# Half of a GELU branch moved ahead of the latent projections in a two-layer mixer kernel

## Chip, core and metric

The kernel runs on one core of a Trainium2 chip. The metric is device time in microseconds (us) of one execution, the median of several runs.

## What is computed

A two-layer network over 512 positions of 1024 channels, followed by a second block. Only layer 1's mixer matters here. It projects the normed input `h` into five pieces and feeds two branches, whose outputs are projected together:

```python
z = h @ w_in
cq, ckv, kr, xr, xg = jnp.split(z, [i1, i2, i3, i4], axis=-1)
q  = (rmsnorm(cq, g_cq) @ w_uq).reshape(Bsz, S, C_HEADS, C_NOPE + C_ROPE)
kv = (rmsnorm(ckv, g_ckv) @ w_ukv).reshape(Bsz, S, C_HEADS, C_NOPE + C_VDIM)
yc = dense_mla(qn, qr, kn, rope(kr), v)
yd = rglru_block(xr, xg, conv_w, conv_b, wa, ba, wx, bx, lam)
return jnp.concatenate([yc, yd], axis=-1) @ w_out
# in rglru_block, for both directions of the recurrence:
r, i = sigmoid(gates of conv(xr)); log_a = -8 * r * softplus(-lam[dirn])
a = exp(log_a); b = sqrt(-expm1(2 * log_a)) * (i * xcf)
h = scan(a, b);  y = (h_forward + h_backward) * gelu(xg)
```

`xr` and `xg` have 512 channels each, `cq` 256, `ckv` 128, `kr` 32. Everything is float32.

## The kernel before

Activations lie transposed: 128 channels on the partitions, 512 positions along the row. A projection block of 128 output channels is 8 chunks of input by 3 matmuls, 24 matmuls of 128x512: each float32 operand is split into a rounded part `hi` (`wh` for weights) and a rest `lo` (`wl`), and `hi*wh + hi*wl + lo*wh` is summed in one PSUM bank (`mm3`, L843). ScalarE or GpSimd makes `hi`, VectorE or GpSimd makes `lo` (`split_to`, L832). GpSimd cannot read PSUM, so what empties a bank is VectorE's or ScalarE's.

One Python program writes the instructions of all five engines in an order of its own: `_Flow` (L368) keeps a planned clock, moves it on by each matmul, and between matmuls lets the tasks that are due emit their next instructions. `_Engine.cost` (L321) holds the planned cost of an instruction, and `copy` and `tt` (L581, L591) put each on the engine that the plan expects to be free first. Tasks marked low go out only when the engines are not far behind. On the chip each engine then runs its own list strictly in order and waits on semaphores; nothing is reordered there.

Layer 1's mixer is phase "c" of the plan, started at L1779. In the order of TensorE's list:

- `xr_blocks` (L1638): four blocks of `xr`, evacuated by VectorE and convolved.
- `lru` (L1691): 16 gate products of three matmuls, each ended by a sigmoid on ScalarE. Behind them `lru_chain` (L1710) runs beside TensorE. `decay` takes two exponentials and a tanh per gate (tiles `la`, `lt`, `sg`) on ScalarE and products on VectorE or GpSimd; then come eight square roots; then `state` runs one scan per channel block and direction on VectorE (eight scans), adds both directions, multiplies by the GELU (tile `ly`) and splits the result.
- `cq.blocks` (two blocks) and `latents` (L1556: one block of `ckv`, one of `kr`). Each latent block is read by ScalarE as `hi` and as a square `sq`, and by VectorE as `lo`.
- `xg_blocks` (L1666): four blocks, each evacuated to `gz` on VectorE; the GELU is then square (ScalarE), `gt` (VectorE), tanh (ScalarE), `gz` again (VectorE).
- `mla_proj` (L1586): keys, queries and values from the latents. Each value block is scaled to `vz` on VectorE and then transposed by TensorE (`v_stack`, L937).

The latents are scaled late. `Latent.scales` (L1537) sums the squares over channels by TensorE (128x1 matmuls, tile `tr`), makes the mean on VectorE in three small instructions (`lt` 128x4), takes the power -0.5 on GpSimd (`pw` 128x4), finishes it on VectorE (`pw<-pw,pw` 128x4), and `bcast_c` (L918) then spreads it over the partitions:

```python
for b in range(NQ):
    tr(ps[:, b * P:(b + 1) * P], r.t[:, b:b + 1].to_broadcast([P, P]), ident)
yield
o.t = blk(name)
V.tensor_copy(o.t, ps)
```

The four transpositions `tr<-cst,pw` stand in TensorE's list wherever the plan expected `r.t` to be there. Nearly all instructions are issued by the helpers, so the trace shows L363 for VectorE, ScalarE and GpSimd, L561 for matmuls, L565 for transpositions. Weights come in units of 1024 columns, two for each block pair; those of this mixer are split during layer 0's MLP and written back to DRAM (`keep_ahead`, L700), and SyncE's queue fetches them (`wh<-wk`, `wl<-wk`) into four buffers in the order of `plan` (L693).

Of the kernel before, what the change touches and what calls it, by code (L numbers as in the profile page):

```python
# [367 lines left out]
class _Flow:  # L368
# [12 lines left out]
    def go(self, gen, low=False):  # L381
        t = _Task(gen, low)
        t.due = self.now + 0.1
        self.tasks.append(t)
        return t
# [89 lines left out]
def _chain(*gens):  # L475
    for g in gens:
        yield from g
# [11 lines left out]
def tile_hybrid(ctx: ExitStack, tc: tile.TileContext, wt, xT, pT, prm_d, cst_d, out):  # L489
# [4 lines left out]
    fl = _Flow()  # L494
# [19 lines left out]
    def blk(name="b", dt=F32, n=T):  # L514
        return bp.tile([P, TB], dt, tag="b", bufs=NB, name=uid(name))[:, 0:n]
# [17 lines left out]
    def take(tag):  # L533
        while (t := bank(tag)) is None:
            yield
        return t
# [6 lines left out]
    def give(tag):  # L543
        banks.append(max(fl.now, fl.last) + 0.1)
        held[tag] -= 1

    def wait(*tasks):
        for t in tasks:
            while not t.done:
                yield  # L550

    def waitc(*tasks):
        for t in tasks:
            while not t.done:
                yield 0.1
# [35 lines left out]
    def tt(op, out, a, b, bias=None):  # L591

        n = width(out)
        if PSUM in (a.space, b.space):
            e = V
        else:
            e = first((V, 0.07 + n / 960.0), (G, 0.07 + n * 0.00227 + (fl.gt if bias is None else bias)))
        e.tensor_tensor(out, a, b, op=op)
# [89 lines left out]
    def unit(name, i):  # L688
        if (name, i) not in units:
            units[name, i] = Unit(name, i, 4 if name == "ein2" else 1)  # L690
        return units[name, i]

    def plan(*names):  # L693
        for nm in names:
            for i in range((_WN[_WT[nm]][1] + 1023) // 1024):
                order.append(unit(nm, i))
# [3 lines left out]
    def keep_ahead(n, *names):  # L700

        us = iter([unit(nm, i) for nm in names for i in range((_WN[_WT[nm]][1] + 1023) // 1024)])

        def chain():
            for u in us:
                if u.task is None and u.raw is None:
                    ahead.append(u)
                    yield from u.keep()

        for _ in range(n):  # L710
            go(chain(), low=True)
# [73 lines left out]
    def PR(name, i=0, n=1):  # L785
        o, w = _PO[name]
        return prm[:, o + i:o + i + n]
# [44 lines left out]
    def split_to(act, ps, scale=None):  # L832
        act.hi, act.lo = blk("hi", F32R), blk("lo", F32R)
        yield from split_ps(ps, act.hi, act.lo, scale)
        yield
        act.done = True

    def mm3g(ps, w, b, nk, mv, m=P, bw=P, base=0, cs=slice(0, T), keep=False):
        for k in range(nk):
            yield from wait(mv[k])  # L840
            yield from mm3(ps, w, base + (b * nk + k) * bw, mv[k], k == 0, k == nk - 1, m, bw, cs, keep)
# [355 lines left out]
    def out_proj(name, yhl, h, then=None, first=None):  # L1197

        for j in range(2):
            w = weights(f"{name}{2 * h + j}")  # L1200
            for b in range(4):
                c = 4 * j + b
                if first is not None:
                    for k in range(NC) if c == 0 else (c + fl.pf,):
                        if k <= c + fl.pf and k < NC:
                            first(k)
                ps = yield from take("mm")
                yield from mm3g(ps, w, b, 4, yhl[4 * h:4 * h + 4])
                while h == 1 and (name, c) not in halves:
                    yield  # L1210
                t = go(residual(c, ps, then, halves[name, c] if h == 1 else None))
                if h == 0:
                    halves[name, c] = t
# [175 lines left out]
    def job0(hd):  # L1389
        st = {}  # L1390

        def score():
# [13 lines left out]
    h, then = next_norm(lambda c: PR("n_mlp0", c), (ss, None))  # L1406
    fill.append(out_proj("eout", yhl, 1, then))
    plan(*[f"m0_{t}_{g}_{i}" for g in range(4) for t in (1, 2) for i in range(4)])
    plan("oin0", "oin1", "lru", "oin4", "oin5", "oin2", "oin3", "ukv0", "uq0", "ukv1", "uq1",
         *[f"oout{i}" for i in range(4)])  # L1410
    fl.finish(fill)

# [56 lines left out]
    def softplus():  # L1469
# [15 lines left out]
        for k in (15, 13, 11, 9, 7, 5, 3, 1):  # L1485
# [14 lines left out]
    go(softplus())  # L1500
    go(masks("m_d4", "m_d16"))
    fl.phase("b")
    keep_ahead(2, "oin0", "oin1", "lru", "oin4", "oin5", "oin2", "oin3", "ukv0", "uq0", "ukv1", "uq1",
                  *[f"oout{i}" for i in range(4)])
    fl.run(mlp(0, h, rb, then))
    h = h2
# [49 lines left out]
    def latents():  # L1556
        yield from ckv.blocks()
        ps = yield from take("mm")
        yield from mm3g(ps, ckv.w, 1, NC, h)

        def evac():
            yield from waitc(rb)
            V.tensor_mul(tk, tk, rb.t)
            V.tensor_mul(tk, ps, tk)
            give("mm")
            yield
            t = blk("kr")
            S.activation(t[0:64], tk[64:128], AF.Copy)
            yield
            V.tensor_add(t[0:64], tk[0:64], t[0:64])  # L1570
            yield
            S.activation(t[64:128], t[0:64], AF.Copy)
            kr.t = t
            yield
            kr.done = True
            yield from waitc(cq.b)
            for i in range(2):
                tt(ALU.mult, tq[i], tq[i], cq.b.t)
            yield
            tqr.done = True  # L1580

        go(evac())
# [55 lines left out]
    def xr_blocks(i):  # L1638
        w = weights(f"oin{i}")
        for b in range(2):  # L1640
            ps = yield from take("mm")
            yield from mm3g(ps, w, b, NC, h)

            def evac(ps=ps, c=2 * i + b):
                yield from waitc(rb)
                xp = blk("xp", n=TB)
                G.memset(xp[:, 0:2], 0.0)
                G.memset(xp[:, T + 2:T + 3], 0.0)
                V.tensor_mul(xp[:, 2:T + 2], ps, rb.t)
                give("mm")  # L1650
                yield
                xc = blk("xc")
                S.activation(xc, xp[:, 0:T], AF.Identity, bias=PR("cb", c), scale=PR("cw", c))
                yield
                for j in range(1, 4):
                    V.scalar_tensor_tensor(xc, xp[:, j:j + T], PR("cw", 4 * j + c), xc,
                                           op0=ALU.mult, op1=ALU.add)
                yield
                a = _Act()
                yield from split_to(a, xc)  # L1660
                xcs[c].t = (xc, a)
                xcs[c].done = True

            go(evac())

    def xg_blocks(i):  # L1666
        w = weights(f"oin{2 + i}")
        for b in range(2):
            ps = yield from take("mm")
            yield from mm3g(ps, w, b, NC, h)  # L1670

            def evac(ps=ps, c=2 * i + b):
                yield from waitc(rb)
                z, t = blk("gz"), blk("gt")
                V.tensor_mul(z, ps, rb.t)
                give("mm")
                yield "low"
                S.activation(t, z, AF.Square, scale=math.sqrt(0.044715))
                yield
                V.scalar_tensor_tensor(t, t, 1.0, z, op0=ALU.add, op1=ALU.mult)  # L1680
                yield
                S.activation(t, t, AF.Tanh, scale=math.sqrt(2.0 / math.pi))
                yield
                V.scalar_tensor_tensor(z, t, 1.0, z, op0=ALU.add, op1=ALU.mult)
                yield
                gelu[c].t = z
                gelu[c].done = True

            go(evac())

    def lru():  # L1691
        wlru = weights("lru")
        gates, ts = {}, []
        for c in range(4):
            yield from wait(xcs[c])
            for d in range(2):
                for t, bn in ((0, "ba"), (1, "bx")):
                    ps = yield from take("mm")
                    yield from mm3g(ps, wlru, c * 4 + d * 2 + t, 1, [xcs[c].t[1]])

                    def evac(ps=ps, k=(c, d, t), b=PR(bn, 4 * d + c)):
                        gates[k] = blk("sg")
                        S.activation(gates[k], ps, AF.Sigmoid, bias=b)
                        give("mm")
                        yield

                    ts.append(go(evac()))
        go(lru_chain(gates, ts), low=True)
# [67 lines left out]
    cq = Latent(256, "oin4", 2, "g_cq", SC96)  # L1776
    ckv = Latent(128, "oin5", 1, "g_ckv", 1.0)
    fl.phase("c")
    fl.run(_chain(xr_blocks(0), xr_blocks(1), lru(), cq.blocks(), latents(), xg_blocks(0), xg_blocks(1)))  # L1779
    fill.extend([mla_proj(1), out_proj("oout", yhl, 0, first=reload(0))])  # L1780
    fl.run(mla_proj(0), fill, 0.0)
    fl.run(attend([job1(i) for i in range(8)], fl.ahead, fl.streams), fill, fl.share)
# [633 lines left out]
```

## Time and profile before

| | before |
|---|---|
| median of 3 runs (lowest, highest) | 1477.36 us (1476.55, 1479.11) |
| the profiled execution: time, span of its records | 1479.96 us, 1478.2 us |
| TensorE busy | 1449.5 us, 98% |
| VectorE busy | 899.0 us, 61% |
| ScalarE busy | 649.5 us, 44% |
| GpSimd busy | 310.7 us, 21% |
| mean granted clock of TensorE | 0.994 |

The busy share of TensorE is high nearly everywhere, so a mean says little. What counts is where its list stands still and which engine it waits for there. The mixer of layer 1 lies between 526 and about 700 us of the span.

### The profile page before, as it was taken

Reading aid. Unit: us, or ns where it says so; the run is one execution under the profiler, and the core shown is the slowest. Engines: PE = TensorE matmul, PEld = TensorE weight load, DVE = VectorE, ACT = ScalarE, POOL = GpSimd, SP = SyncE. Lnnn points to the kernel's source line nnn. Section 1 sums busy time; section 2 is a strip of 40 time slices with the busy share of each in tenths; the row PEclk is TensorE's granted clock in tenths of the full one; section 3 lists DMA queues with packets and bytes.
Section 4 is the critical chain, followed back from the end, with each engine's and each line's share of the span. In section 5 each row is a group of like instructions: output and inputs, shape, how many; then the busy total and the mean of one; then the engine's idle time right before and its main releaser. Section 6 shows DMA issues by size and latency. Waiting matters only on the chain.

```text
span 1478.2 us, 18891 instructions
## 1 busy us (share of the span) xinstructions
PE 1449.5 (98%) x6789; PEld 1174.4 (79%) x6789; DVE 899.0 (61%) x1410; ACT 649.5 (44%) x1192; POOL 310.7 (21%) x291
## 2 busy tenths in 40 slices
PE   8999999999999999899999999999999999999998
PEld 5777878888888888688888888888787788888787
DVE  7896864655434555977775665657755566536413
ACT  5684432433222347487433434334521576324623
POOL 5451220211102013631120210202110000100332
PEclk9999999999999999999999999999999999999999
DMA  6113588888423454333499999999865223346252
GB/s 212 52 44 99 176 291 272 286 290 280 133 95 100 137 213 158 127 129 128 149 318 330 327 330 330 314 336 323 287 216 195 109 86 115 115 182 214 103 196 89
DMA packets 118317, 291.44 MB, mean 197 GB/s; under 512 B 13136, under 2 KB 14672, under 8 KB 118224
## 3 DMA queue, kind: packets, MB, share of 16 engines
q1 hardware_dynamic: 118080, 289.98, 57.9%
q8 instruction: 53, 0.87, 0.2%
q14 instruction: 40, 0.33, 0.1%
q10 hardware_dynamic: 144, 0.26, 0.1%
HBM read 205.26 MB, written 84.93 MB: 196 GB/s over the span
## 4 chain that ended last, share of the span: by engine, by line
PE 83%; DMA 7%; DVE 5%; issue 1%; ACT 1%; SPq 1%; POOL 0%; DVEq 0%; POOLq 0%; ACTq 0%
PE mm L561 72%; PE sc L561 4%; PE av L561 3%; PE tr L565 3%; DMA kr<-in_wt_dram 3%; DMA wk<-klo 2%; PE tr L561 1%; DMA wk<-khi 1%; DVE wl L363 1%; DMA x<-in_xT_dram 1%; ACT wh L363 1%; DVE klo L363 0%; DVE gz L363 0%; DVE sg L363 0%; DMA pin<-in_pT_dram 0%
## 5 line engine op out<-in xcount | busy, mean ns | idle before, releaser
L561 PE MATMUL mm<-hi,wh 128*128 128x512 f32 (+1 forms) x1276 | 509.4, 399 | 0.8 <-POOL wh L363 0.5
L561 PE MATMUL mm<-hi,wl 128*128 128x512 f32 (+1 forms) x1276 | 501.1, 393 | 4.4 <-DVE wl L363 2.6
L561 PE MATMUL mm<-lo,wh 128*128 128x512 f32 (+1 forms) x1276 | 499.3, 391 | 0.3 <-POOL lo L363 0.3
L561 PEld LDWEIGHTS mm<-lo,wh 128*128 128x128 f32 x1276 | 240.4, 188 | 55.6 <-POOL lo L363 0.8
L561 PEld LDWEIGHTS mm<-hi,wl 128*128 128x128 f32 x1276 | 240.8, 189 | 54.9 <-DVE wl L363 3.6
L561 PEld LDWEIGHTS mm<-hi,wh 128*128 128x128 f32 x1276 | 240.9, 189 | 52.9 <-ACT wh L363 1.5
L363 ACT ACTIVATE khi<-kr 128x512 fp32r<-128x512 f32 x120 | 75.8, 632 | 308.8 <-DMA kr<-in_wt_dram 303.1
L561 PE MATMUL mm<-ul,wh 128*128 128x512 f32 x512 | 201.6, 394 | 1.8 <-DVE ul L363 1.8
L561 PE MATMUL mm<-uh,wh 128*128 128x512 f32 x512 | 201.7, 394 | 0.3 <-ACT uh L363 0.3
L561 PE MATMUL mm<-uh,wl 128*128 128x512 f32 x512 | 201.6, 394 | 0.0
L363 DVE TENSOR_TENSOR wl<-wr,wh 128x1024 fp32r<-128x1024 f32 (+1 forms) x145 | 184.5, 1273 | 6.4 <-ACT wh L363 4.8
L363 DVE TENSOR_TENSOR klo<-kr,khi 128x512 fp32r<-128x512 f32 x150 | 124.3, 830 | 87.7 <-ACT khi L363 77.3
L363 ACT ACTIVATE wh<-wr 128x1024 fp32r<-128x1024 f32 (+1 forms) x147 | 148.8, 1013 | 47.8 <-PE mm L561 34.4
L363 DVE TENSOR_TENSOR x<-x,mm 128x512 f32<-128x512 f32 x112 | 76.8, 686 | 151.0 <-PE mm L561 146.3
L363 POOL TENSOR_TENSOR ma<-ma 128x512 f32<-128x512 f32 x62 | 85.4, 1377 | 282.7 <-ACT uh L363 232.2
L561 PEld LDWEIGHTS mm<-ul,wh 128*128 128x128 f32 x512 | 96.2, 188 | 25.2 <-DVE ul L363 2.9
L561 PEld LDWEIGHTS mm<-uh,wh 128*128 128x128 f32 x512 | 96.1, 188 | 23.1 <-ACT uh L363 0.7
L561 PEld LDWEIGHTS mm<-uh,wl 128*128 128x128 f32 x512 | 96.2, 188 | 22.3
L363 ACT ACTIVATE p<-sc,nm 128x512 f32<-128x512 f32 (+3 forms) x136 | 75.2, 557 | 30.4 <-DVE nm L363 27.3
L363 DVE TENSOR_TENSOR pl<-tr,ph 128x512 fp32r<-128x512 f32 (+2 forms) x108 | 66.5, 623 | 25.4 <-ACT ph L363 24.8
L363 POOL TENSOR_SCALAR khi<-kr 128x512 fp32r<-128x512 f32 x30 | 28.6, 953 | 250.3 <-DMA kr<-in_wt_dram 214.1
L363 DVE SCALAR_TENSOR_TENSOR ma<-mm,rb 128x512 f32<-128x512 f32 x64 | 44.1, 688 | 52.4 <-PE mm L561 52.2
(290 smaller groups left out, 1619.0 us busy)
## 6 DMA issues: line engine op xcount, KB each, us to landing
wr<-in_wt_dram SPq DMA_DIRECT2D x144, 512.0 KB, 5.3
kr<-in_wt_dram SPq DMA_DIRECT2D x150, 256.0 KB, 5.9
wk<-khi SPq DMA_DIRECT2D x150, 256.0 KB, 5.9
wk<-klo SPq DMA_DIRECT2D x150, 256.0 KB, 5.7
wh<-wk SPq DMA_DIRECT2D x74, 512.0 KB, 3.3
wl<-wk SPq DMA_DIRECT2D x74, 512.0 KB, 4.2
x<-xs SPq DMA_DIRECT2D x16, 256.0 KB, 5.1
cst<-in_cst_dram SPq DMA_DIRECT2D x8, 256.0 KB, 5.4
```

Source lines behind the costliest of these rows:

```text
L363: return fn(*a, **k)
L561: PE.matmul(o, l, r, start=start, stop=stop, skip_group_check=True)
L565: PE.transpose(o, i, idn)
```

## The change

The chain of projections at L1779 takes `xg_blocks(0)`, two of the four `xg` blocks, in front of `cq.blocks()` and `latents()`. The two lists that set the order of the weights follow it: `oin2` (weights of these two blocks) comes before `oin4` (`cq`) and `oin5` (`ckv`, `kr`).

```diff
-    plan("oin0", "oin1", "lru", "oin4", "oin5", "oin2", "oin3", "ukv0", "uq0", "ukv1", "uq1",
+    plan("oin0", "oin1", "lru", "oin2", "oin4", "oin5", "oin3", "ukv0", "uq0", "ukv1", "uq1",
...
-    keep_ahead(2, "oin0", "oin1", "lru", "oin4", "oin5", "oin2", "oin3", "ukv0", "uq0", "ukv1", "uq1",
+    keep_ahead(2, "oin0", "oin1", "lru", "oin2", "oin4", "oin5", "oin3", "ukv0", "uq0", "ukv1", "uq1",
...
-    fl.run(_chain(xr_blocks(0), xr_blocks(1), lru(), cq.blocks(), latents(), xg_blocks(0), xg_blocks(1)))
+    fl.run(_chain(xr_blocks(0), xr_blocks(1), lru(), xg_blocks(0), cq.blocks(), latents(), xg_blocks(1)))
```

The planner then writes all lists anew from this point. No engine's list differs ahead of the first block behind the gates. Three places of them:

TensorE, around the first transposition that spreads a latent scale (`tr<-cst,pw`; `mm_5046` is the first `xg` block before, `mm_5130` the third `xg` block in the change). Before, it stands in the middle of the first `xg` block, with three and a half blocks behind it up to the keys:

```order
L561 MATMUL mm_5046<-hi_4305,wl_4872 128x512
L561 MATMUL mm_5046<-lo_4306,wh_4871 128x512
L565 MATMUL tr_5056<-cst,pw_5023 128x128 x4
L561 MATMUL mm_5046<-hi_4343,wh_4871 128x512
L561 MATMUL mm_5046<-hi_4343,wl_4872 128x512
```

Now:

```order
L561 MATMUL mm_5130<-hi_4423,wl_5022 128x512
L561 MATMUL mm_5130<-lo_4424,wh_5021 128x512
L565 MATMUL tr_5160<-cst,pw_5134 128x128 x4
L561 MATMUL mm_5130<-hi_4461,wh_5021 128x512
L561 MATMUL mm_5130<-hi_4461,wl_5022 128x512
```

Counted from the first block behind the gates, 102 matmuls and both sums of squares stand ahead of the first transposition before, and 159 matmuls and both sums now. The second transposition now stands 9 matmuls further on.

VectorE, around the last step of the same scale (`pw<-pw,pw`), which those transpositions read. Scans print as SCALAR_TENSOR_TENSOR `sg<-la,sg`. Before, both scales are finished and copied (`bc`) ahead of the first scan:

```order
L363 SCALAR_TENSOR_TENSOR pw_5023<-pw_5023,pw_4583 128x4
L363 TENSOR_TENSOR cst_4526<-cst_4526,rb_4599 128x512
L363 TENSOR_TENSOR cst_4526<-mm_4976,cst_4526 128x512
L363 SCALAR_TENSOR_TENSOR pw_5044<-pw_5044,pw_4583 128x4
L363 COPY bc_5065<-tr_5056 128x512
L363 COPY bc_5077<-tr_5067 128x512
L363 TENSOR_TENSOR kr_5072<-cst_4526,kr_5072 64x512
L363 SCALAR_TENSOR_TENSOR sg_4728<-la_4835,sg_4720 128x512
L363 TENSOR_TENSOR gz_5102<-mm_5046,rb_4599 128x512
```

Now the first scale comes behind the last of the eight scans (`sg_4827` is the eighth):

```order
L363 TENSOR_TENSOR cst_4526<-mm_5059,cst_4526 128x512
L363 SCALAR_TENSOR_TENSOR sg_4827<-la_4908,sg_4821 128x512
L363 SCALAR_TENSOR_TENSOR ly_5143<-sg_4728,gz_4883 128x512
L363 TENSOR_TENSOR sg_4787<-sg_4787,sg_4795 128x512
L363 SCALAR_TENSOR_TENSOR pw_5134<-pw_5134,pw_4583 128x4
L363 SCALAR_TENSOR_TENSOR ly_5155<-sg_4755,gz_4934 128x512
L363 COPY bc_5170<-tr_5160 128x512
L363 TENSOR_TENSOR kr_5165<-cst_4526,kr_5165 64x512
L363 SCALAR_TENSOR_TENSOR pw_5148<-pw_5148,pw_4583 128x4
L363 COPY bc_5201<-tr_5188 128x512
```

From the first scan up to `pw_5134` the list holds the eight scans, nine instructions of 128x512 and six of 128x4.

ScalarE, at the last of the square roots (`sg_4805` and `sg_4821` below). The reads of the second `cq` block (`mm_4976`) and of `ckv` (`mm_5025`) stood ahead of the roots before, and now stand behind them:

```order
 L363 ACTIVATE sg_4805<-sg_4805 128x512
 L363 ACTIVATE sg_4821<-sg_4821 128x512
-L363 ACTIVATE kr_5072<-cst_4526 64x512
-L363 ACTIVATE kr_5072<-kr_5072 64x512
-L363 ACTIVATE gt_5103<-gz_5102 128x512
+L363 ACTIVATE hi_5029<-mm_4976,prm 128x512
+L363 ACTIVATE sq_5035<-mm_4976 128x512
+L363 ACTIVATE hi_5064<-mm_5025,prm 128x512
+L363 ACTIVATE sq_5072<-mm_5025 128x512
```

In the place of four of these reads, ahead of the roots, the squares and tanhs of two GELU blocks have come in.

## Rows read from the trace of the kernel before

**Rows 1.** The page's part 1: busy us (share of span) and instructions.

```profile
PE 1449.5 (98%) x6789; PEld 1174.4 (79%) x6789; DVE 899.0 (61%) x1410; ACT 649.5 (44%) x1192; POOL 310.7 (21%) x291
```

**Rows 2.** TensorE's waits, whole span: waiter, releaser: us in total, times, longest.

```profile
PE tr L565 <- DVE vz L363: 7.5, 3, 6.7
```

**Rows 3.** TensorE's timeline: start, us, instruction, [idle before <-releaser].

```profile
607.79 0.39 PE L561 MATMUL mm<-lo,wh 128*128 128x512 f32 x1
614.86 1.12 PE L565 MATMUL tr<-cst,vz 128*128 128x128 f32 x4 [6.68 <-DVE vz L363]
...
617.88 0.39 PE L561 MATMUL mm<-lo,wh 128*128 128x512 f32 x1
```

**Rows 4.** Busy us by stretch: PE, PEld, DVE, ACT, POOL; granted clock, DMA share, GB/s.

```profile
612.00:614.00 2.00, 0.00 (x0) 0.00 (x0) 2.00 (x3) 1.94 (x4) 2.00 (x2) 0.50 0.00 0
...
618.00:619.00 1.00, 1.00 (x6) 0.83 (x5) 1.00 (x3) 0.51 (x1) 1.00 (x2) 1.00 0.57 180
```

**Rows 5.** The chain that ended last, 529 to 575 us: start, us, what.

```profile
529.70 44.52 PE mm L561 x192
574.22 0.78 PE tr L561 x8
```

**Rows 6.** ScalarE's timeline behind the decays.

```profile
572.92 0.68 ACT L363 ACTIVATE hi<-mm,prm 128x512 fp32r<-128x512 f32 x1
573.49 0.59 ACT L363 ACTIVATE sq<-mm 128x512 f32<-128x512 f32 x1
574.10 1.28 ACT L363 ACT_TABLE_LOAD   x1
575.40 4.27 ACT L363 ACTIVATE sg<-sg 128x512 f32<-128x512 f32 x8
```

**Rows 7.** VectorE's timeline, scales and scans.

```profile
564.65 0.75 DVE L363 SCALAR_TENSOR_TENSOR lo<-mm,prm,hi 128x512 fp32r<-128x512 f32 x1 [11.51 <-ACT sq L363]
...
575.54 0.16 DVE L363 TENSOR_TENSOR lt<-pw 128x4 f32<-128x4 f32 x1
...
576.08 0.15 DVE L363 TENSOR_TENSOR lt<-pw 128x4 f32<-128x4 f32 x1
...
582.50 1.21 DVE L363 TENSOR_TENSOR_SCAN sg<-la,sg 128x512 f32<-128x512 f32 x1
584.57 0.69 DVE L363 TENSOR_TENSOR gz<-mm,rb 128x512 f32<-128x512 f32 x1 [0.86 <-PE mm L561]
585.18 1.95 DVE L363 TENSOR_TENSOR_SCAN sg<-la,sg 128x512 f32<-128x512 f32 x1
587.06 1.72 DVE L363 TENSOR_TENSOR sg<-sg,sg 128x512 f32<-128x512 f32 x1
...
592.37 3.31 DVE L363 TENSOR_TENSOR_SCAN sg<-la,sg 128x512 f32<-128x512 f32 x2
...
596.19 2.32 DVE L363 TENSOR_TENSOR_SCAN sg<-la,sg 128x512 f32<-128x512 f32 x1
...
599.72 1.22 DVE L363 TENSOR_TENSOR_SCAN sg<-la,sg 128x512 f32<-128x512 f32 x1
600.86 0.67 DVE L363 TENSOR_TENSOR sg<-sg,sg 128x512 f32<-128x512 f32 x1
```

**Rows 8.** GpSimd's timeline beside the scans.

```profile
580.74 1.29 POOL L363 TENSOR_TENSOR cst<-cst,bc 128x512 f32<-128x512 f32 x1
581.99 6.23 POOL L363 TENSOR_TENSOR sg<-sg,sg 128x512 f32<-128x512 f32 x3
591.83 1.65 POOL L363 TENSOR_TENSOR sg<-sg,sg 128x512 f32<-128x512 f32 x1 [3.61 <-DVE sg L363]
595.76 1.67 POOL L363 TENSOR_TENSOR sg<-sg,sg 128x512 f32<-128x512 f32 x1 [2.28 <-DVE sg L363]
```

**Rows 9.** VectorE's timeline: the first and second value evacuation.

```profile
614.12 0.68 DVE L363 TENSOR_TENSOR vz<-mm,bc 128x512 f32<-128x512 f32 x1
...
619.64 0.68 DVE L363 TENSOR_TENSOR vz<-mm,bc 128x512 f32<-128x512 f32 x1
```

## The prediction
> **What bounds the kernel now.** The page's first part comes first: TensorE is busy 98% of the span [rows 1], so time can only be won or lost where its list stands still. The waits of TensorE show where: the transposition `tr<-cst,vz` waited 7.5 us for VectorE's `vz`, 6.7 of it in one piece [rows 2]. TensorE's own timeline puts that piece at the first value block of the MLA projections: the last matmul starts at 607.79, the next instruction at 614.86, 6.68 us idle [rows 3]. The granted clock stands at 0.50 (1.2 GHz) by 612 to 614, and is back at 1.00 (2.4 GHz) in the stretch that starts at 618.00 [rows 4]; the timeline has the matmuls at their old pace from 617.88 [rows 3], so the slow piece behind the stall is 617.88 - 614.86 = 3.0 us long and costs about half of that, 1.5 us.
>
> Why is `vz` late? VectorE's timeline shows it: from the first scan at 582.50 it works with hardly a gap (one of 0.86 us) [rows 7], and `vz` is simply its turn at 614.12 [rows 9]. Earlier it had stood still for 11.51 us, until 564.65, because ScalarE was busy with the decays and had not yet read the first latent block [rows 7]. So the stage has a VectorE queue that starts late and a TensorE list that needs its results early. The change touches both.
>
> **What it takes away.** The GELU work of two blocks (`gz`, `gt`, `gz` each: six instructions of VectorE) moves from behind the scans to the stretch before them, where VectorE idled. At some 0.60 us from start to start (585.18 - 584.57 [rows 7]) that is 3.6 us less in front of `vz`. Two of the four `xg` blocks no longer stand between the latents and the keys. I take the old 6.68 us stall as gone or nearly so, because the new list makes TensorE wait earlier for something else, and VectorE catches up meanwhile.
>
> **What it adds: when TensorE gets to the scale.** The page of waits has nothing on the new wait, so I build it from both sides. Before, the first sum of squares starts at 574.22 [rows 5]; 87 matmuls stand between the first block behind the gates and that point (three blocks and 15). In the change 159 matmuls and both sums stand ahead of the first `tr<-cst,pw`. A matmul takes 44.52 / 192 = 0.232 us, and each of the two sums 0.78 [rows 5]. TensorE gets there at 574.22 + 72 x 0.232 + 2 x 0.78 = 592.5.
>
> **When the scale is ready.** ScalarE first. Ahead of the roots four latent reads (two `hi`, two `sq`) give way to two squares and two tanhs. From start to start a read takes 0.57 and 0.61, and a step on a whole tile without a scale, such as a root, 4.27 / 8 = 0.53 [rows 6]: four of either differ by 0.2 us, which I leave out. The load of the root table stays at 574.10 and the roots end at 575.40 + 4.27 = 579.7 [rows 6]. Only then come `hi` and `sq` of the second `cq` block, 1.2 us, to 580.8, and VectorE's `lo` of that block waits for them (the row at 564.65 shows that `lo` is released by `sq`). With 0.6 for `lo` the first scan starts at 581.4, only 1.1 us earlier than before; VectorE idles ahead of it once more.
>
> Now the length of the queue in front of `pw<-pw,pw`. Before, from 582.50 to 600.86 VectorE did eight scans and seven instructions of 128x512 in 18.36 us, 0.86 of it idle: 17.5 us [rows 7]. The new list has eight scans, nine such instructions and two trios of small ones: 17.5 + 2 x 0.60 + 2 x 0.54 (a trio takes 576.08 - 575.54 [rows 7]) = 19.8 us.
>
> GpSimd comes on top. VectorE instructions that read two SBUF tiles are stretched when one of GpSimd runs: a scan lasts 1.21 us alone and 1.95 beside it, 2.32 and 3.31 (for two) further on, a product 1.72 against 0.67 [rows 7, 8]. The excesses are 0.74 and 1.10 for the single scans, 1.05 for the product and 0.95 for the pair (3.31 less 1.14 and 1.22), together 3.84 us for the five GpSimd instructions there [rows 7, 8]. The new list gives GpSimd seven in the stretch (the sum of squares is one of the new ones): two more, 2 x 0.77 = 1.5 us. Sum: 21.3 us, the scale is ready at 602.7, and with 0.2 us for the last small step TensorE starts at 602.9.
>
> **New stall: 602.9 - 592.5 = 10.4 us.** Bounds: with no stretching at all (eight scans at 600.86 - 599.72 = 1.14 [rows 7], nine at 0.60, small ones 1.1, four hand-overs of 0.1) the queue is 16.0 us and the stall 5.1. With eight GpSimd instructions at the largest excess seen, 1.10, it is 16.0 + 8.8 = 24.8 and 13.9. I take 10.4, since the measured stretch has nearly the same contents.
>
> The Trainium skill, "SBUF — State Buffer", section "Who interferes with whom", says that a VectorE instruction with two SBUF inputs and a GpSimd one that reads SBUF contend for a port pair under an exclusive lock: whoever is first holds it for its whole instruction and the other is blocked fully. By that rule the sum would be rival 3's where GpSimd is always first. The rows agree with it in kind, and their mean excess is smaller.
>
> **Behind the stall.** The clock will fall as it did at the old one; I book the same 3.0 us slow piece, so 1.5 us on both sides, no difference. The second scale needs its power (GpSimd, long done) and four more VectorE instructions, about 3.5 us, while TensorE has nine matmuls at the slow clock, 3.9 us: no wait. In the MLA projections VectorE's queue per value block does not shrink: 614.12 to 619.64, 5.5 us, before [rows 9]; TensorE needs 21 matmuls and a transposition, 5.2 us at full clock. Before, the slow clock hid part of that, and the two later waits were 7.5 - 6.7 = 0.8 us [rows 2]. In the change these blocks run at full clock: I add 0.7 us (between 0 and 1.5). SyncE's queue issues the same fetches with two names exchanged, each behind the same matmul count: nothing. Layer 0's MLP splits the same units: nothing.
>
> **Sum.** New waits 10.4 + 0.8 + 0.7 = 11.9 us, old ones 7.5 us: +4.4 us. The profiled execution took 1479.96 us and would take 1484.4; it lies 2.6 us above the median of the runs shown (1477.36), so the median to expect is 1481.8 us.
>
> **Rivals.**
> (1) *The wait only changes place.* If VectorE's queue runs with little stretching, the new stall is 5.1 to 8.9 us and the sum between -1.6 (5.1 + 0.8 - 7.5, the later waits not grown) and +2.9 us (8.9 + 0.8 + 0.7 - 7.5): 1475.8 to 1480.3. For it: GpSimd loses the port in part of the overlaps (three of its instructions took 6.23 us, 2.4 more than 3 x 1.29 [rows 8]). Against: the measured 17.5 us are a whole stretch of this very work. A change within 0.2%, which is about what a measurement of this kernel can tell from none, is 3.0 us. Also here belongs that the move does nothing because other things hide it.
> (2) *Faster.* VectorE's idle time is filled, the old stall of 6.68 us and its slow 1.5 us go, and the scale comes in time. It decides at the transposition: for a gain over 3.0 us the stall plus the 1.5 us of later waits must stay under 4.5 us, so the stall under 3.0, and the queue under 592.5 + 3.0 - 581.4 - 0.2 = 13.9 us. At zero the time would be 1477.4 - 7.5 - 1.5 + 1.5 = 1469.9 us, with later waits grown by 1.5. Against it: even without stretching the rows give 16.0 us.
> (3) *VectorE loses every meeting* with GpSimd and stands for the whole of its instruction, 1.29 us where nothing held it up [rows 8]: the queue is 16.0 + 7 x 1.29 = 25.0 us, the stall 14.1, the sum +8.1 and the time 1485.5 us. For it: three of the four excesses are near 1 us; against: their mean over five GpSimd instructions is 0.77. This is the case that the rule cited above would give.
> (4) *The clock stays low longer* after the longer idle: every further 3.0 us at 1.2 GHz add 1.5 us, 1483.3.
>
> **How the numbers follow.** Forecast (the stall moves and grows, +3 to +6.5 us): 0.58. Rival 3: 0.06. Rival 4: 0.05. Rival 1: 0.25. Rival 2: 0.06. Slower by over 0.2% is the forecast with 3 and 4, 0.69; within is 0.25; faster 0.06. The range goes from the lower part of rival 1, 1477.5, to rival 3's 1485.5: below it lie rival 2 and a quarter of rival 1, above it little.
>
> **What would show it.** TensorE's waits should list `tr<-cst,pw` (or L565) waiting about 10 us for VectorE's `pw`, starting near 592.5, with the clock at 0.50 behind it, and no wait of several us before the first `tr<-cst,vz`. VectorE should start its first scan near 581.4 after an idle of 6 us or more released by ScalarE's `sq`, and have the eight scans and `ly` ahead of `pw`. The prediction is wrong if VectorE reaches `pw<-pw,pw` before 598, if the first scan starts before 579, or if a wait of over 3 us is left at the values.

## The result, and the profile after

The changed kernel takes 1486.04 us (median of 5 runs, 1485.1 to 1489.73), the kernel before in the same comparison 1477.88 us. The ratio is 1.0059 with a 95% interval of 1.0038 to 1.0080: slower by 8.2 us, between 5.6 and 11.8. The forecast was slower by 4.4 us; the direction came, the time lies 0.5 us above the range.

The page's part 1 of the changed kernel; every busy time is within 5 us of [rows 1], so nearly all of the loss is idle time again (of the 6.1 us by which the two profiled executions differ, TensorE's busy time has 0.9):

```profile
PE 1450.4 (98%) x6789; PEld 1175.5 (79%) x6789; DVE 899.7 (61%) x1409; ACT 650.3 (44%) x1193; POOL 315.3 (21%) x291
```

TensorE's waits, whole span. They answer to [rows 2]: one wait for `pw` has come in, and the waits for `vz` are down from 7.5 to 2.8 us:

```profile
PE tr L565 <- DVE pw L363: 12.1, 1, 12.1
PE tr L565 <- DVE vz L363: 2.8, 3, 1.5
```

TensorE's timeline shows where (start, us, instruction, idle before and its releaser). The wait stands where the prediction put it, at the first transposition that spreads a latent scale, and the matmuls behind it come 0.43 us apart until 607.59 instead of 0.23. At the values the old stall [rows 3] is gone; the row above counts three small waits there, of which the longest is 1.5 us:

```profile
590.31 0.39 PE L561 MATMUL mm<-lo,wh 128*128 128x512 f32 x1
602.84 1.11 PE L565 MATMUL tr<-cst,pw 128*128 128x128 f32 x4 [12.14 <-DVE pw L363]
...
607.16 0.63 PE L561 MATMUL mm<-lo,wh 128*128 128x512 f32 x1
607.59 0.81 PE L565 MATMUL tr<-cst,pw 128*128 128x128 f32 x4
...
608.48 0.39 PE L561 MATMUL mm<-hi,wl 128*128 128x512 f32 x1
```

Busy times by stretch (PE, PEld, DVE, ACT, POOL, then granted clock, DMA share, GB/s): the clock falls between 594 and 595, stands at 0.50 (1.2 GHz) from 595 to the end of the wait and under the first matmuls behind it, and is back at 608, as [rows 4] had it behind the old stall. From 595 to 600 VectorE is busy 95% of the time:

```profile
594.00:595.00 1.00, 0.00 (x0) 0.00 (x0) 1.00 (x2) 0.00 (x0) 1.00 (x2) 0.68 0.00 0
595.00:600.00 5.00, 0.00 (x0) 0.00 (x0) 4.75 (x9) 0.66 (x2) 2.68 (x3) 0.50 0.00 0
...
607.00:608.00 1.00, 1.00 (x4) 0.70 (x4) 0.00 (x0) 0.00 (x0) 0.00 (x0) 0.50 0.00 0
608.00:610.00 2.00, 2.00 (x12) 1.69 (x11) 1.56 (x3) 0.24 (x1) 0.79 (x1) 0.99 0.56 153
```

ScalarE reads the second `cq` block only behind the eight roots, which answers to [rows 6]:

```profile
573.36 4.28 ACT L363 ACTIVATE sg<-sg 128x512 f32<-128x512 f32 x8
577.55 0.67 ACT L363 ACTIVATE hi<-mm,prm 128x512 fp32r<-128x512 f32 x1
578.12 0.58 ACT L363 ACTIVATE sq<-mm 128x512 f32<-128x512 f32 x1
```

VectorE idles 5.81 us for that `sq`, then starts the scans at 579.40 and gets to `pw<-pw,pw` at 601.53, behind all eight scans [rows 7 show the same work before]:

```profile
578.73 0.75 DVE L363 SCALAR_TENSOR_TENSOR lo<-mm,prm,hi 128x512 fp32r<-128x512 f32 x1 [5.81 <-ACT sq L363]
579.40 1.75 DVE L363 TENSOR_TENSOR_SCAN sg<-la,sg 128x512 f32<-128x512 f32 x1
581.07 1.72 DVE L363 TENSOR_TENSOR sg<-sg,sg 128x512 f32<-128x512 f32 x1
...
594.60 1.16 DVE L363 TENSOR_TENSOR lt<-pw 128x4 f32<-128x4 f32 x1
...
599.86 1.75 DVE L363 TENSOR_TENSOR sg<-sg,sg 128x512 f32<-128x512 f32 x1
601.53 1.25 DVE L363 SCALAR_TENSOR_TENSOR pw<-pw,pw 128x4 f32<-128x4 f32 x1
```

GpSimd beside it; each of these 128x512 instructions has a stretched one of VectorE next to it:

```profile
580.02 6.08 POOL L363 TENSOR_TENSOR sg<-sg,sg 128x512 f32<-128x512 f32 x3
...
594.28 1.45 POOL L363 TENSOR_TENSOR sg<-sg,sg 128x512 f32<-128x512 f32 x1
...
599.43 1.62 POOL L363 TENSOR_TENSOR sg<-sg,sg 128x512 f32<-128x512 f32 x1 [1.75 <-DVE sg L363]
601.02 1.73 POOL L363 TENSOR_TENSOR lo<-ly,hi 128x512 fp32r<-128x512 f32 x1
```

One execution reaches the mixer a few microseconds earlier or later than another, so the stage is best timed between two marks of TensorE's own list. The first is the transposition that spreads layer 1's input scale, the second the first sum of squares of the next norm. Before:

```profile
529.10 0.60 PE L565 MATMUL tr<-cst,pw 128*128 128x128 f32 x4
...
1089.19 0.95 PE L561 MATMUL tr<-onec,sq 128*128 128x1 f32 x8
```

In the change:

```profile
527.11 0.60 PE L565 MATMUL tr<-cst,pw 128*128 128x128 f32 x4
...
1095.13 0.95 PE L561 MATMUL tr<-onec,sq 128*128 128x1 f32 x8
```

560.1 us before, 568.0 in the change: in the two profiled executions the change costs 7.9 us between the marks, nearly all of the 8.2 us between the medians. I call this "the stage" below, and a time of the change has 2.0 us added (529.10 - 527.11) where it is held against one of before.

### The profile page after: what moved, and what is told of

Same layout as the page of the kernel before. It is cut to its first block, busy times and chain, and to the rows that moved or that the text cites. A ratio compares the mean times of both kernels' runs of the same rounds, so it can differ in the third digit from the quotient of the medians.

```text
span 1484.3 us, 18893 instructions
## 1 busy us (share of the span) xinstructions
PE 1450.4 (98%) x6789; PEld 1175.5 (79%) x6789; DVE 899.7 (61%) x1409; ACT 650.3 (44%) x1193; POOL 315.3 (21%) x291
## 4 chain that ended last, share of the span: by engine, by line
PE 81%; DMA 7%; DVE 6%; ACT 3%; issue 1%; SPq 1%; POOL 0%; DVEq 0%; POOLq 0%; ACTq 0%
PE mm L561 69%; DMA kr<-in_wt_dram 5%; PE sc L561 4%; PE tr L565 3%; PE av L561 3%; DVE sg L363 1%; DVE wl L363 1%; PE tr L561 1%; ACT sg L363 1%; ACT wh L363 1%; DMA wk<-khi 1%; DVE lo L363 1%; DVE klo L363 1%; DMA wk<-klo 0%; ACT la L363 0%
```

## The experiments

All ratios are to the kernel before, measured on the same chip. The changed kernel stands at 1.0059 and a stage of 568.0 us, the kernel before at 560.1 us. A stage is that of the one profiled execution of its kernel, and how much it varies between executions of one kernel is not known. Outside the marks the thirteen profiled executions took 916.6 to 922.2 us, so an effect of a few us can show in the stage and be lost in the time.

| edit | stage, us | ratio [95% interval] |
|---|---|---|
| change, spread later | 563.3 | 1.0019 [1.0008, 1.0029] |
| change, scale ahead of the scans | 565.5 | 1.0040 [1.0026, 1.0055] |
| change, no GpSimd in the recurrence | 564.7 | 1.0038 [1.0024, 1.0053] |
| change, a scan booked at 2.2 us | 566.7 | 1.0041 [1.0026, 1.0056] |
| change, wait filled with matmuls | 566.0 | 1.0053 [1.0041, 1.0065] |
| before, wait filled with matmuls | 560.7 | 1.0017 [1.0008, 1.0025] |
| before, no GpSimd in the recurrence | 558.5 | 1.0000 [0.9992, 1.0009] |
| all four blocks ahead | 560.4 | 1.0010 [0.9999, 1.0021] |
| all four ahead, no GpSimd | 555.2 | **0.9974 [0.9962, 0.9985]** |
| change, spread later, no GpSimd | 559.0 | 1.0000 [0.9991, 1.0009] |
| one block ahead | 569.9 | 1.0068 [1.0054, 1.0082] |

### The transpositions later in TensorE's list

```diff
-            go(bcast_c(self.b, self.r))
+            go(self.spread())
+
+        def spread(self):
+            yield from waitc(xg_all)
+            yield from bcast_c(self.b, self.r)
...
+            xg_all.done = (i, b) == (1, 1)
```

> The changed kernel, with the transpositions that spread both latent scales held back in TensorE's list until the fourth xg block is issued; VectorE's list is the same up to the scale. 63 matmuls instead of 27 stand between the first sum of squares and the first transposition, 36 x 0.232 = 8.4 us more work ahead of it. Theory A (TensorE reaches the scale too early for a VectorE queue that is as long as before): the scale is ready at the same 602.8, the 12.1 us wait shrinks to 4 to 6 us (the last one read may be the second scale, 1.5 us later), the time falls by 6 to 8 us to about 1479. Rival B (the weights' new order, the clock or a slower queue behind the stall makes the loss): the time stays at 1484 or more.

TensorE's timeline:

```profile
604.18 1.97 PE L565 MATMUL tr<-cst,pw 128*128 128x128 f32 x8 [4.47 <-DVE pw L363]
...
609.79 0.59 PE L561 MATMUL mm<-hi,wh 128*128 128x512 f32 x1
610.22 0.41 PE L561 MATMUL mm<-hi,wl 128*128 128x512 f32 x1
```

The wait fell from 12.14 to 4.47 us, inside A's 4 to 6, and rival B (1484 or more) fell: the time is 1481.7. It is not 1479, though. The stage is 4.7 us shorter than the change's, not 6 to 8, and 3.2 us longer than before. One reason is in the rows: the matmuls behind this shorter wait stay slow for 5.9 us (604.18 to some 610.1), against 3.0 us before [rows 3]; at a little under half each that is 1.3 us. The rest is not traced to one wait.

### The scale ahead of the scans on VectorE

```diff
             yield from split_to(yhl[c], y)
 
+        yield from waitc(cq.r, ckv.r)
         for c in range(4):
             go(state(c), low=True)
```

> The changed kernel, with the recurrence's states (products, scans, sums) held back in the lists until both latent scales are finished, so that the scale stands ahead of the first scan on VectorE. Theory A, with the queue as the cause: the wait for pw is gone, the first scan starts about 10 us later (near 590), VectorE idles ahead of it, and the same queue now stands in front of the values: waits of 5 us or more at vz or at a PSUM bank, time 1481 to 1486. Rival C (only the scale's place in VectorE's list is at fault): no wait of more than 3 us is left, time 1475 or less.

VectorE's first scans, then TensorE's longest wait:

```profile
594.60 2.32 DVE L363 TENSOR_TENSOR_SCAN sg<-la,sg 128x512 f32<-128x512 f32 x2
```

```profile
621.37 1.11 PE L565 MATMUL tr<-cst,vz 128*128 128x128 f32 x4 [4.95 <-DVE vz L363]
```

The wait for `pw` is gone and the scans start 13 us later than in the change (594.60 against 579.40, less 2.1 us between the first marks), where about 10 was expected. The same queue now stands ahead of the values: 4.95 us for `vz`, 2.5 for `gz`, 1.7 without a named releaser. 1484.6 us is within A's 1481 to 1486; rival C (1475 or less) fell. Where the scale stands decides where TensorE waits; of how much it waits, 10.9 of the change's 14.9 us are left.

### The recurrence without GpSimd

```diff
-                tt(ALU.mult, b, b, ig)
+                V.tensor_tensor(b, b, ig, op=ALU.mult)
...
-            tt(ALU.add, hs[0], hs[0], hs[1])
+            V.tensor_tensor(hs[0], hs[0], hs[1], op=ALU.add)
```

> The changed kernel, with the recurrence's products and sums all on VectorE (six of them were on GpSimd). Between the first scan and the first scale VectorE then has eight scans, 14 instructions of 128x512 instead of 9, and six small ones. Theory D (what stretches the queue is GpSimd beside it, some 0.9 us for each meeting): 8 x 1.14 + 14 x 0.60 + 1.5 = 19.0 us and one or two meetings left, about 20 instead of 23.4 us; the wait for pw falls from 12.1 to 8 to 10 us, the time to 1481 to 1484. Rival E (the stretching is VectorE's own, GpSimd costs it nothing): five more instructions make the queue 3 us longer, the wait 15 us, the time 1488 to 1490.

VectorE's timeline:

```profile
584.90 1.22 DVE L363 TENSOR_TENSOR_SCAN sg<-la,sg 128x512 f32<-128x512 f32 x1
...
592.23 0.14 DVE L363 TENSOR_TENSOR lt<-pw 128x4 f32<-128x4 f32 x1
...
600.83 0.14 DVE L363 SCALAR_TENSOR_TENSOR pw<-pw,pw 128x4 f32<-128x4 f32 x1
```

TensorE's:

```profile
601.02 1.12 PE L565 MATMUL tr<-cst,pw 128*128 128x128 f32 x4 [7.21 <-DVE pw L363]
```

With more instructions the queue is shorter. From 581.81, the first product, to `pw` at 600.97 it takes 19.2 us instead of 23.4, and all eight scans take 1.22 or 1.23 us. That is near D's 20, but D counted 14 instructions of 128x512 and the trace has twelve there, against nine in the change: at D's prices 8 x 1.14 + 12 x 0.60 + 1.5 = 17.8 us without any meeting. Of the 1.4 us on top, 0.55 are the one meeting left, the first product beside GpSimd's sum of squares (1.22 instead of 0.67 us). The wait is 7.2 us, a little below D's 8 to 10, the time 1484.2 us, at D's upper end. Rival E (15 us, 1488 to 1490) fell. The time fell less than the wait, since the other waits (for `qz` 2.3, for `vz` 1.2, for `pl` 0.9 us) came in place of 2.8 us for `vz`.

### One number of the planner

```diff
+        if name == "tensor_tensor_scan":
+            return 2.2
         if name in ("tensor_scalar", "tensor_copy", "memset"):
```

> The changed kernel, with one number of the planner changed: a scan is booked at 2.2 us instead of the 0.60 of any 128x512 instruction (the trace has 1.1 to 2.2 for one). The blocks stand in the same order; only where the plan puts the transpositions and the scale between the rest moves: five scans instead of eight stand ahead of the first scale, 30 matmuls instead of 27 ahead of its transposition, 21 instead of 9 up to the second. Theory A: the scale is ready near 593, the wait for pw is 3 us or less, later waits sum to 4 to 8 us, time 1478 to 1483. Rival B (the loss lies in the order of the blocks itself): 1485 or more.

TensorE's timeline:

```profile
593.91 0.65 PE L567 MATMUL tr<-cst,pw 128*128 128x128 f32 x4 [1.68 <-DVE pw L365]
...
627.73 1.12 PE L567 MATMUL tr<-cst,vz 128*128 128x128 f32 x4 [4.66 <-DVE vz L365]
...
640.54 0.48 PE L563 MATMUL sc<-hi,hi 128*128 128x512 f32 x1 [3.01 <-DVE v L365]
```

The scale came when A said and the wait for it was 1.7 us. But the later waits sum to 10.4 us instead of 4 to 8, and 1484.85 us lies between A's 1483 and B's 1485: it tells neither. Together with the second experiment it shows that a wait which is planned away comes back downstream for the most part, as long as VectorE has as much to do: all waits of the mixer sum to 12.1 us here and 10.9 there, against 14.9 in the change.

### The clock's share

48 matmuls that nothing reads, in the wait of the changed kernel:

```diff
         ps = yield from takec("tr")
+        for _ in range(warm_n[0] if name == "bc" else 0):
+            PE.matmul(ps, h[0].hi[:, 0:P], h[0].hi, start=True, stop=True, skip_group_check=True)
+        warm_n[0] = 0 if name == "bc" else warm_n[0]
         for b in range(NQ):
             tr(ps[:, b * P:(b + 1) * P], r.t[:, b:b + 1].to_broadcast([P, P]), ident)
...
+    warm_n[0] = 48
```

> The changed kernel, with 48 matmuls of 128x512 in TensorE's list right in front of the first transposition tr<-cst,pw; they write the bank that the transposition then overwrites, and nothing reads them. Every other list is the same. They last 48 x 0.232 = 11.1 us and lie in the wait of 12.1 us. Theory F (the clock's fall is a cost of its own behind the wait: 4.8 us of matmuls at 0.50 in the changed kernel): about 1 us of the wait is left, the scale is ready at the same time, the granted clock stays at 1.00, and the time falls by 2.0 to 2.5 us to about 1484. Rival G (the low clock costs nothing, since the stage waits for VectorE anyway): the later waits for vz grow by as much, 1486.

TensorE's timeline, then the stretch 593 to 606 in the same columns as above:

```profile
599.78 4.24 PE L925 MATMUL tr<-hi 128*128 128x512 f32 x18
...
605.34 0.65 PE L565 MATMUL tr<-cst,pw 128*128 128x128 f32 x4 [1.31 <-DVE pw L363]
```

```profile
593.00:606.00 13.00, 11.69 (x54) 9.45 (x53) 12.45 (x17) 1.35 (x3) 8.25 (x6) 1.00 0.05 18
```

The clock stayed at 1.00, the waits for `vz` stayed at 2.8 us, and the stage is 2.0 us shorter, which is F's 2.0 to 2.5 and not G. The medians do not resolve it: 1485.98 against the changed kernel's 1486.04, with intervals that overlap. So F rests on one profile.

The same in the kernel before, in `v_stack` ahead of its first transposition:

```diff
         ps = yield from takec("tr")
+        for _ in range(warm_n[0]):
+            PE.matmul(ps, warm_s[0].hi[:, 0:P], warm_s[0].hi, start=True, stop=True, skip_group_check=True)
+        warm_n[0] = 0
         for b in range(NQ):
             tr(ps[:, b * P:(b + 1) * P], z[:, b * P:(b + 1) * P], ident)
...
+    warm_n[0] = 24
+    warm_s.append(cq.a[0])
```

> The kernel before, with 24 such matmuls in front of its first tr<-cst,vz, whose wait is 6.68 us: 24 x 0.232 = 5.6 us of it are filled. Theory F: the clock stays at 1.00, 1.5 us less, 0.999 of the kernel before. Rival G: no change.

VectorE's first two value evacuations, which answer to [rows 9]:

```profile
612.96 0.68 DVE L363 TENSOR_TENSOR vz<-mm,bc 128x512 f32<-128x512 f32 x1
...
618.48 0.68 DVE L363 TENSOR_TENSOR vz<-mm,bc 128x512 f32<-128x512 f32 x1
```

F fell here. This execution runs 1.17 us ahead of the one before (its first mark stands at 527.93), and with that added VectorE evacuates at 614.13 and 619.65, to 0.01 us as before. The clock was up, and TensorE only waited the gain away at the next values: 3.1 us in three waits instead of 0.8 in two. The stage is 0.6 us longer, the median 2.0 us; what made the rest of that is open. By these profiles the slow piece was hidden behind VectorE's work in the kernel before and not in the change; with one profile of each that is likely and not shown.

### GpSimd in the kernel before

The diff is that of the third experiment, on the kernel before.

> The kernel before, with the recurrence's products and sums all on VectorE. Theory D (a GpSimd instruction beside VectorE costs it about 0.9 us, and the same product on VectorE costs 0.60): five more instructions of 0.60 are less than the 3.84 us of stretching that go, so vz comes 1 to 2 us earlier, the wait falls from 6.7 to 4.5 to 6 us, the time by 1 to 2 us. Rival E (no stretching by GpSimd): vz 3 us later, wait 9.7 us, time 3 us longer.

```profile
612.43 1.03 PE L565 MATMUL tr<-cst,vz 128*128 128x128 f32 x4 [4.22 <-DVE vz L363]
```

TensorE's wait for the first `vz` is 4.22 instead of 6.68 us, a little below D's 4.5 to 6, and the stage 1.6 us shorter; E (3 us longer) fell. The medians do not differ (1.0000, interval 0.9992 to 1.0009), so of the 1 to 2 us in time at most 1.2 can be there.

### All four blocks ahead, and one

```diff
-    ... lru(), xg_blocks(0), cq.blocks(), latents(), xg_blocks(1)))
+    ... lru(), xg_blocks(0), xg_blocks(1), cq.blocks(), latents()))
```

In the two lists of weights `oin3` moves in front of `oin4` accordingly.

> The changed kernel, with all four xg blocks in front of the latent projections instead of two (weights in the same order). Theory A (what counts is how far VectorE's queue has come when TensorE reaches the scale): TensorE gets there some 11 us later, when all scans are done, so it waits for the sums and the scale's own steps only, 5 to 8 us in pieces, time 1477 to 1482. Rival H (each xg block that is moved costs 4 us): 1494.

```profile
595.11 1.87 PE L561 MATMUL tr<-onec,sq 128*128 128x1 f32 x8 [3.54 <-DVE sq L363]
...
605.20 0.39 PE L561 MATMUL mm<-lo,wh 128*128 128x512 f32 x1
```

1479.64 us is in A's range, far from H's 1494. TensorE waits 3.5 us for a sum of squares that VectorE adds behind its scans, 1.4 for a `vz`, and never for `pw`. The clock stays low until the second row, so the slow piece is 10.1 us long (595.11 to 605.20), the longest behind any wait in these runs. The times of this kernel spread widest, 1476.3 to 1485.3 us, and the profiled execution (1477.0) is one of the fastest.

Half of the move, one block:

```diff
-    def xg_blocks(i):
+    def xg_blocks(i, bs=(0, 1)):
...
-    ... lru(), xg_blocks(0), cq.blocks(), latents(), xg_blocks(1)))
+    ... lru(), xg_blocks(0, (0,)), cq.blocks(), latents(), xg_blocks(0, (1,)), xg_blocks(1)))
```

> One xg block ahead of the latent projections instead of two. The first latent's scale (cq) then stands ahead of the first scan on VectorE, the second one's (ckv) behind all eight, and 39 matmuls stand between their transpositions. Theory A: no wait of over 3 us at the first scale, but the second is as late as in the changed kernel: 8 to 11 us there, time 1482 to 1486, nearly the whole loss from half of the move. Rival H (each block costs 4 us): half of the loss, 1481 to 1482, in many small waits.

```profile
579.01 1.08 PE L565 MATMUL tr<-cst,pw 128*128 128x128 f32 x4 [2.63 <-DVE pw L363]
...
600.62 1.11 PE L565 MATMUL tr<-cst,pw 128*128 128x128 f32 x4 [9.51 <-DVE pw L363]
```

Both scales cost a wait, 2.63 and 9.51 us, each with slow matmuls behind it. One block costs 1.0068, two 1.0059, four 1.0010: no price per block. H fell; A gave the second wait, but its 1482 to 1486 was too little by 2.5 us: it had the first wait without a fall of the clock, and the transpositions behind it took 1.08 us where they take 0.60 at 1.00.

### What beats both

All four blocks ahead and the recurrence on VectorE, the diffs of the eighth and the third run together:

> All four xg blocks ahead of the latent projections (as in the run before) and the recurrence's products and sums on VectorE (as in the two runs on GpSimd). With all four ahead TensorE's list gives VectorE the longest time for the scans, and what was left was a wait of 3.5 us for a sum of squares that VectorE added behind scans stretched by GpSimd. Theory D: without the stretching that wait falls to about 1 us, all waits of the mixer to 2 to 5 us with no fall of the clock, against 7.5 us and a slow piece before: 2 to 4 us less than the kernel before, 0.997 to 0.999. Rival E: as without this edit, 1.001.

TensorE's waits from 520 to 735 us, all of them:

```profile
PE tr L561 <- POOL sq L363: 1.0, 1, 1.0
PE av L561 <- DVE pl L363: 0.2, 1, 0.2
PE tr L565 <- DVE vz L363: 0.2, 1, 0.2
```

1474.28 us, ratio 0.9974 with an interval wholly under 1: 3.8 us less than the kernel before and some 12 less than the change. The waits are smaller than D's 2 to 5 us. One part of the expectation failed: the clock did fall once, for 3 us, behind the wait of 1.0 us:

```profile
592.00:593.00 1.00, 1.00 (x4) 0.81 (x3) 0.96 (x2) 0.00 (x0) 0.00 (x0) 0.50 0.00 0
```

This run's gain is therefore not the waits' alone. The eighth run had 5.1 us of waits and 10.1 us of slow matmuls, this one has 1.4 and some 3; the stage is 5.2 us shorter. How the gain divides between the two is not shown.

The changed order with the diffs of the first and the third run together:

> The changed kernel with both of its repairs: the spreading transpositions behind the fourth xg block (as in the first run) and the recurrence's products and sums on VectorE. Theory A with D: TensorE reaches the scale near 599, the scale is ready near 600, so the wait for pw is 2 us or less and the clock does not fall there; the rest of the queue then stands in front of the values as in the kernel before, a wait of 3 to 5 us for vz. Time within 2 us of the kernel before. Rival B (the order of the blocks costs by itself): 1482 or more.

```profile
602.83 1.09 PE L565 MATMUL tr<-cst,pw 128*128 128x128 f32 x8 [0.24 <-DVE pw L363]
...
615.51 0.66 PE L565 MATMUL tr<-cst,vz 128*128 128x128 f32 x4 [3.26 <-DVE vz L363]
```

Each wait is where it was expected, and the time is that of the kernel before. The fair partner is the kernel before without GpSimd in the recurrence: stage 559.0 against 558.5 us, both at a ratio of 1.0000. So the order of the blocks costs next to nothing by itself (B fell); what it cost was a scale that VectorE reached late and TensorE asked for early.

## Why the prediction was right in kind and too small

*Where and when.* Right. With the 2.0 us added, the first scan starts at 581.4 (predicted 581.4), and TensorE's last matmul ahead of the wait ends its step near 592.7 (predicted 592.5). The wait is at `tr<-cst,pw`, the old stall at `vz` is gone, ScalarE's `sq` behind the roots is what VectorE idles for (5.81 us, "6 us or more" was said). The first experiment shows the mechanism: with VectorE's list as it was up to the scale, work moved in front of the transposition shrinks the wait.

*The queue.* This step failed most: 21.3 us were booked, 601.53 + 1.25 - 579.40 = 23.4 measured, so the wait was 12.1 instead of 10.4 us, +1.7. The eight scans and the rest without GpSimd would take 16.0 us by the lower bound, so some 7.4 us are stretching; the excesses, added up row by row over the stretch, are 7.1 us. Two things were short in "two more, 2 x 0.77". An eighth GpSimd instruction was left out, the split `lo<-ly,hi` at 601.02, which the list has beside the scale itself. And I took the excess from scans and products alone: the small instructions `lt<-pw` and `pw<-pw,pw` went in at their free price, but took 1.16 and 1.25 us beside GpSimd, against 0.14 each without it (third experiment). Those two alone are 2.1 us. The mean excess of a meeting came to 7.1 / 8 = 0.9 us, against the 0.77 booked. By the Trainium skill, "SBUF — State Buffer", section "Who interferes with whom", an instruction of VectorE with two SBUF inputs contends under an exclusive lock with one of GpSimd that reads SBUF; the rule names no size. The rows agree: both of these small ones have two SBUF inputs (`lt<-pw` reads one tile twice), and both were held. Rival 3's full price was not reached. Its queue of 25.0 us counted seven meetings; with the eighth it would be 16.0 + 8 x 1.29 = 26.3 us, and eight at the booked mean give 16.0 + 8 x 0.77 = 22.2, which is nearer to 23.4. That rival 3's time, 1485.5 us, is the nearest of all to 1486.04 is luck: it had too long a stall, 14.1 us, and neither the longer waits at the values nor the longer slow piece.

*Later waits.* "I add 0.7 us" failed: the waits at the values were 2.8 us, not 1.5. I had read VectorE's time per value block from the first one alone, 5.5 us [rows 9]; the next `vz` of the kernel before stood at 626.85, another 7.2 us on. In the change the first step is 6.5 us (620.19 to 626.71). Before:

```profile
626.85 0.67 DVE L363 TENSOR_TENSOR vz<-mm,bc 128x512 f32<-128x512 f32 x1
```

In the change:

```profile
620.19 0.68 DVE L363 TENSOR_TENSOR vz<-mm,bc 128x512 f32<-128x512 f32 x1
...
626.71 0.68 DVE L363 TENSOR_TENSOR vz<-mm,bc 128x512 f32<-128x512 f32 x1
```

*The slow piece.* "I book the same 3.0 us slow piece" failed: it was 607.59 - 602.84 = 4.8 us. At 0.43 instead of 0.23 us for a matmul a slow piece loses 46% of its length, so 2.2 us against 1.4: +0.8. The fifth run's 2.0 us agrees.

*Sum.* 4.4 + 1.7 + 1.3 + 0.8 = 8.2 us, which is the difference of the medians. The terms come from one profile of each kernel, whose stages differ by 7.9 us, and the difference of the medians is known only to between 5.6 and 11.8, so that the two agree to 0.1 us is luck. The range missed by 0.5 us because its upper end moved only the stall: later waits and the slow piece kept one value each in every case, though the first had a bound of 1.5 us of its own. Rivals 1 and 2 were excluded by the stall alone; rival 4's slow piece did come out longer, by 1.8 us instead of the 3.0 that it priced, but its reason, the longer idle, is not borne out: the first experiment has 5.9 us behind a wait of 4.47. At the range's lower end, 1477.5 us, 1.7 of rival 1's 4.5 us lie below it and not a quarter; the result does not touch that end.

*The faster rival.* Its premise, that VectorE's idle time before the scans is filled and the backlog shrinks by as much, held only in part: VectorE still idled 5.81 us ahead of the first scan. The version that is faster needed the move taken further and the stretching taken out.

## What to carry to other kernels

When a block of matmuls is moved ahead of another, look for the last small instruction in another engine's list that TensorE's next step reads, and count what stands ahead of it there and how many matmuls TensorE has until then: the difference is the wait. A wait that is only planned elsewhere comes back for the most part at a later step while the engine behind it has as much to do; it went away here when the queue itself got shorter (products taken off GpSimd) and TensorE's list asked later. Price every 128x512 instruction of GpSimd (here products, sums and splits of SBUF tiles) that may run beside a list of VectorE instructions with two SBUF inputs at about 0.9 us on top of that list, once for each GpSimd instruction (0.77 in the kernel before, 0.9 in the change), also where the instruction that it meets is small.

## What the runs showed that I had not expected

- A VectorE instruction of 128x4 is held as long as one of 128x512: 1.16 and 1.25 us beside GpSimd's 128x512 instructions, 0.14 without, so 1.0 and 1.1 us on top, as with the products at 581.07 and 599.86 (1.72 and 1.75 instead of 0.67). GpSimd's own 128x4 power did not do this: at 592.92 in the third experiment it ran 1.40 us beside a scan of 1.22.
- The slow piece behind a wait does not grow with the wait: 3.0 us behind 6.68, 5.9 behind 4.47, 10.1 behind 3.54 (all four blocks ahead), 4.8 behind 12.14.
- The clock fell behind a wait of 1.03 us at a sum of squares (the run that beats both), but stayed at 1.00 behind one of 1.68 us between full matmuls (the fourth experiment). Why is open.
